# A final norm without GpSimd products: one more residual sum on the tensor engine, and the eight tiles in a new order

## The chip, the core and the metric

The kernel runs on one core of one Trainium2 chip. The metric is the time of one execution on the device in microseconds (us); the figure to be moved is the median of repeated executions.

## What is computed

One layer of a diffusion backbone on 1024 latent tokens of width 1024 (a token mixer, then an expert-choice mixture of 16 experts), and at the end an RMS norm. What matters here is the end: the experts' outputs are summed into the tokens, and each token is normed.

```python
def expert_choice_ffn(h, w_r, w1, w3, w2):
    ...
    gate, idx = lax.top_k(jnp.swapaxes(aff, 1, 2), cap)      # cap = 128 tokens for each expert
    xe = h[bidx, idx]
    hid = jax.nn.silu(jnp.einsum('becd,edf->becf', xe, w1)) * jnp.einsum('becd,edf->becf', xe, w3)
    ye = jnp.einsum('becf,efd->becd', hid, w2) * gate[..., None].astype(h.dtype)
    return jnp.zeros_like(h).at[bidx, idx].add(ye)

def rmsnorm(x, g):
    xf = x.astype(jnp.float32)
    y = xf * lax.rsqrt(jnp.mean(xf * xf, axis=-1, keepdims=True) + EPS)
    return (y * g.astype(jnp.float32)).astype(x.dtype)

x = x + g2x * expert_choice_ffn(hx2, w_router[l], w1[l], w3[l], w2[l])
...
return rmsnorm(x, final_g)
```

## The kernel before

Nearly all of the time goes to the 16 experts, one after the other. Their weights stream in over one DMA queue as pieces of 1 MB (tile `raw`); ScalarE (ACT) rounds each piece to `hi` (line 107), VectorE (DVE) takes the rest as `lo` (line 109), and TensorE (PE) multiplies both with the split activations (`up`, lines 1258 to 1262, and `down`, lines 1301 to 1307). The outputs of experts 0 to 14 are scattered into the token array `x2d` in DRAM by an indirect DMA that adds (line 1317). Each engine works its queue in the order in which the program is written, and waits on semaphores in between.

The last expert is treated otherwise, and its end is what the change touches. While it still runs, the four pieces of `x2d` (two tiles of 128 tokens each) are loaded into `xf` (line 1386). Its output `ye` is split into `yh` (ACT, line 1393) and `yl` (DVE, line 1394). Then each of the eight tiles `t` of 128 tokens by 1024 goes through four steps:

- `spread(t, add)`: PE multiplies a one-hot matrix `ohT` with `yh` and `yl` (lines 1406 and 1407), so that the expert's rows land at their tokens, in two PSUM banks `fp` of 512 columns. With `add`, PE puts the token's own row `xf` in first, through a product with the identity (line 1405), and the sum `x` then stands in PSUM. There are six banks of this kind, so three tiles can be in them at a time.
- `residual(t)`: for tiles without `add`, DVE adds the two banks to `xf` (line 1414, twice 128x512).
- `square(t)`: ACT squares and sums the row (line 1424) and takes the root (line 1429, with line 1428 ahead of it where the row comes in two halves).
- `finish(t)`: DVE takes the reciprocal `r` (line 1441) and writes the output `fo`, which SP's queue stores (line 1449). There are two ways to write it: `scalar_tensor_tensor` computes `x * r * fg` in one instruction (line 1448); or, where `gains(t)` has had GpSimd (POOL) multiply `x` by the gains `fg` (line 1436), DVE only multiplies by `r` with a `tensor_scalar` (line 1446).

Before, tiles 2, 3 and 4 have their sum made on PE, tiles 0, 1, 5, 6 and 7 on DVE, and tiles 1, 5, 6 and 7 have their gains product on GpSimd. Nothing but the order of the calls at the end of the program sets the order of the work.

Of the kernel before, what the change touches and what calls it, by code (L numbers as in the profile page):

```python
# [7 lines left out]
F32 = mybir.dt.float32  # L8
# [4 lines left out]
OP = mybir.AluOpType  # L13
# [3 lines left out]
D = 1024  # L17
# [3 lines left out]
P = 128  # L21
# [24 lines left out]
def hybrid_layer(ctx, tc, x, c, ctxt, c_ctx, w_mod, b_mod, norm1_g, norm2_g, w_in, sgu_g, sgu_w,  # L46
# [3 lines left out]
    V, A, PE, G = nc.vector, nc.scalar, nc.tensor, nc.gpsimd  # L50
# [19 lines left out]
    def bank(shape, name, small=0):  # L70
        return banks[small].tile(shape, F32, name=name, tag="bk")

    def raw(shape, dt, name):
        return rawp.tile(shape, dt, name=name, tag="raw")
# [96 lines left out]
    ident = con.tile([P, P], F32, name="ident")  # L171
# [129 lines left out]
    for k in range(8):  # L301
        hi = p0.tile([P, 2048], F32R, name="mhi", bufs=2)
        lo = p0.tile([P, 2048], F32R, name="mlo", bufs=2)
        for c0, n_ in (((0, 4),) if k < 7 else ((0, 1), (1, 1), (2, 1), (3, 1))):
            sl = slice(c0 * 512, (c0 + n_) * 512)
            A.activation(hi[:, sl], wm0[k][:, sl], AF.Copy)
            V.tensor_sub(lo[:, sl], wm0[k][:, sl], hi[:, sl])
            for w in (hi, lo):
                for n in range(c0, c0 + n_):
                    PE.matmul(pm[n], cs4[:, k, :], w[:, n * 512:(n + 1) * 512],  # L310
                              start=(k == 0 and w is hi), stop=(k == 7 and w is lo))
# [18 lines left out]
    for j in range(16):  # L330
# [8 lines left out]
                           op0=OP.add, op1=OP.mult)  # L339
# [204 lines left out]
    XS = {}  # L544
# [299 lines left out]
    p = bank([P, 4, P], "ws")  # L844
# [304 lines left out]
    for h in range(2):  # L1149
        sl = slice(h * 512, (h + 1) * 512)  # L1150
# [195 lines left out]
    for e in range(NE):  # L1346
# [24 lines left out]
        else:  # L1371
# [5 lines left out]
            fg = mp.tile([P, D], F32, name="fg", tag="xe", bufs=2)  # L1377
# [13 lines left out]
    for n in range(2):  # L1391
        sl = slice(n * 512, (n + 1) * 512)
        A.activation(yh[:, sl], ye[:, sl], AF.Copy)
        V.tensor_sub(yl[:, sl], ye[:, sl], yh[:, sl])
    FP, XS = {}, {}

    def spread(t, add):

        v = xf[t // 4][:, t % 4]
        FP[t] = [bank([P, 512], "fp") for _ in range(2)]  # L1400
        for n in range(2):
            sl = slice(n * 512, (n + 1) * 512)
            p = FP[t][n]
            if add:
                PE.matmul(p, ident, v[:, sl], start=True, stop=False)
            PE.matmul(p, ohT[:, t * P:(t + 1) * P], yh[:, sl], start=not add, stop=False)
            PE.matmul(p, ohT[:, t * P:(t + 1) * P], yl[:, sl], start=False, stop=True)
        if add:
            XS[t] = FP[t]

    def residual(t):
        v = xf[t // 4][:, t % 4]
        for n in range(2):
            V.tensor_add(v[:, n * 512:(n + 1) * 512], v[:, n * 512:(n + 1) * 512], FP[t][n])
        XS[t] = [v]

    fo = {}

    def square(t):
        if t not in fo:  # L1420
            fo[t] = raw([P, 2, D], F32, "fo")
        w = D // len(XS[t])
        for n, v in enumerate(XS[t]):
            A.activation(fo[t][:, 1, n * w:(n + 1) * w], v, AF.Square, accum_out=fs[:, n, t:t + 1])
        m = epst
        if len(XS[t]) > 1:
            m = fs[:, 0, t:t + 1]
            A.activation(m, m, AF.Identity, bias=epst, scale=1.0 / D)
        A.activation(fs[:, 2, t:t + 1], fs[:, len(XS[t]) - 1, t:t + 1], AF.Sqrt, bias=m, scale=1.0 / D)

    GM = set()

    def gains(t):

        fo[t] = raw([P, 2, D], F32, "fo")
        G.tensor_tensor(fo[t][:, 0], XS[t][0], fg, op=OP.mult)
        GM.add(t)

    def finish(t):
        o, r = fo[t][:, 0], fs[:, 2, t:t + 1]  # L1440
        V.reciprocal(r, r)
        w = D // len(XS[t])
        for n, v in enumerate(XS[t]):
            sl = slice(n * w, (n + 1) * w)
            if t in GM:
                V.tensor_scalar(o, o, r, None, op0=OP.mult)
            else:
                V.scalar_tensor_tensor(o[:, sl], v, r, fg[:, sl], op0=OP.mult, op1=OP.mult)
        nc.sync.dma_start(out[t * P:(t + 1) * P], o)

    for t, add in ((0, False), (1, False), (5, False), (2, True), (3, True)):
        spread(t, add)
    residual(0)
    square(0)
    residual(1)
    gains(1)
    square(1)
    finish(0)
    residual(5)
    gains(5)  # L1460
    spread(6, False)
    spread(7, False)
    square(2)
    finish(1)
    square(5)
    finish(2)
    spread(4, True)
    residual(6)
    gains(6)
    square(3)  # L1470
    finish(5)
    finish(3)
    square(6)
    residual(7)
    gains(7)
    finish(6)
    square(4)
    finish(4)
    square(7)
    finish(7)  # L1480


# [29 lines left out]
```

## Time and profile before

| | us |
|---|---|
| median of 3 runs | 1621.77 |
| lowest and highest | 1614.16, 1622.4 |
| the profiled execution | 1619.82 |
| its span | 1617.7 |
| PE busy, share of the span | 1531.9 (95%) |
| DVE busy | 1386.6 (86%) |
| ACT busy | 1089.8 (67%) |
| POOL busy | 144.6 (9%) |

A profile is of one execution. The span runs from its first to its last recorded instruction, and 2.1 us lie around it. Times inside the trace count from the span's start. The busy shares are means over the whole span; the stretch that the change touches is the last 32 us, and there the shares are others. In a timeline a row gives an instruction's start and how long it took, and in square brackets how long its engine had been idle and what ended that. [...]

### The profile page before, as it was taken

How to read it: one execution, taken by the hardware profiler on the slowest of the kernel's cores; microseconds unless marked ns; L12 is line 12 of the kernel's file. 1: busy time of each engine (PE TensorE's matmuls, PEld its weight loads, DVE VectorE, ACT ScalarE, POOL GpSimd, SP SyncE). 2: the span in 40 equal slices, each digit the busy share in tenths (PEclk: the TensorE clock that was granted, in tenths of full speed). 3: DMA queues.
4: the chain of work that ended last, by engine and by line, in shares of the span. 5: the costliest groups of instructions: out<-in, count | busy, mean ns of one | idle time of the engine just before them, and what ended most of it. 6: DMA issues, size and time to landing. Idle time of an engine off the chain costs nothing.

```text
span 1617.7 us, 19119 instructions
## 1 busy us (share of the span) xinstructions
PE 1531.9 (95%) x7288; PEld 1257.4 (78%) x7288; DVE 1386.6 (86%) x1322; ACT 1089.8 (67%) x990; POOL 144.6 (9%) x126
## 2 busy tenths in 40 slices
PE   5899989999769999999999999999999999999996
PEld 2687779888657888888888888888888888887784
DVE  6668788886878898998989889898998989889797
ACT  6577654722347877777777777868777787777873
POOL 2411121000010010010100001010010100001002
PEclk8899999998879999999999999999999999999998
DMA  9110147435659999999999999999999999999855
GB/s 383 35 36 30 66 151 228 171 127 207 233 214 357 381 375 356 396 366 397 381 365 381 372 378 381 380 385 357 387 370 388 387 371 373 370 384 377 325 173 207
DMA packets 85947, 485.30 MB, mean 300 GB/s; under 512 B 11224, under 2 KB 20064, under 8 KB 35680
## 3 DMA queue, kind: packets, MB, share of 16 engines
q1 hardware_dynamic: 80896, 466.72, 74.9%
q0 software_dynamic: 4864, 17.34, 4.3%
q8 instruction: 57, 0.93, 0.2%
q14 instruction: 34, 0.28, 0.0%
q10 hardware_dynamic: 96, 0.03, 0.0%
HBM read 463.61 MB, written 20.45 MB: 299 GB/s over the span
## 4 chain that ended last, share of the span: by engine, by line
PE 67%; DVE 16%; ACT 7%; DMA 7%; issue 3%; POOL 1%; SPq 0%; DVEq 0%; POOLq 0%; ACTq 0%
PE h L1258 12%; PE h L1262 12%; PE h L1260 12%; PE ye L1304 7%; PE ye L1301 7%; PE ye L1307 7%; DMA raw<-in_w_dram 3%; DVE lo L109 3%; ACT hi L107 2%; PE hp L1285 2%; DVE ring L404 1%; DMA ring<-in_w_mod_dram 1%; DVE sg L1279 1%; PE pw L925 1%; PE pw L927 1%
## 5 line engine op out<-in xcount | busy, mean ns | idle before, releaser
L109 DVE TENSOR_TENSOR lo<-raw,hi 128x2048 fp32r<-128x2048 f32 x383 | 871.0, 2292 | 116.3 <-ACT hi L107 112.1
L107 ACT ACTIVATE hi<-raw 128x2048 fp32r<-128x2048 f32 x384 | 737.3, 1922 | 215.5 <-PE h L1262 150.9
L1258 PE MATMUL h<-hi,xth 128*128 128x512 f32 x1024 | 292.6, 400 | 3.6 <-ACT sg L1269 1.2
L1260 PE MATMUL h<-lo,xth 128*128 128x512 f32 x1024 | 279.9, 390 | 1.9 <-DVE lo L109 1.9
L1262 PE MATMUL h<-hi,xtl 128*128 128x512 f32 x1024 | 279.7, 390 | 0.0
L1258 PEld LDWEIGHTS h<-hi,xth 128*128 128x128 f32 x1024 | 187.8, 188 | 50.6 <-DVE sg L1279 12.6
L1260 PEld LDWEIGHTS h<-lo,xth 128*128 128x128 f32 x1024 | 192.4, 188 | 42.6 <-DVE lo L109 2.8
L1262 PEld LDWEIGHTS h<-hi,xtl 128*128 128x128 f32 x1024 | 192.4, 188 | 40.6
L1301 PE MATMUL ye<-hi,hth 128*128 128x512 f32 x512 | 158.0, 390 | 0.0
L1304 PE MATMUL ye<-lo,hth 128*128 128x512 f32 x512 | 157.8, 389 | 0.0
L1307 PE MATMUL ye<-hi,htl 128*128 128x512 f32 x512 | 157.6, 389 | 0.0
L1317 POOL DMA_INDIRECT x2d<-ye,ix x15 | 50.6, 3374 | 790.0 <-DVE ye L1314 790.0
L1304 PEld LDWEIGHTS ye<-lo,hth 128*128 128x128 f32 x512 | 96.0, 188 | 20.3 <-DVE lo L109 0.3
L1307 PEld LDWEIGHTS ye<-hi,htl 128*128 128x128 f32 x512 | 96.1, 188 | 20.0
L1301 PEld LDWEIGHTS ye<-hi,hth 128*128 128x128 f32 x512 | 95.8, 188 | 19.6
L1269 ACT ACTIVATE sg<-h 128x512 f32<-128x512 f32 x64 | 69.7, 1109 | 0.1
L1288 ACT ACTIVATE hth<-hp 128x512 fp32r<-128x512 f32 x64 | 35.0, 596 | 42.3 <-PE hp L1285 42.3
L377 PE MATMUL pu<-hxh,wh 128*128 128x512 f32 x128 | 51.0, 399 | 1.0 <-ACT g1row L738 1.0
L1236 POOL DMA_INDIRECT xe<-hx2d,ix x16 | 17.7, 1106 | 382.9 <-DVE gate L1231 367.5
L379 PE MATMUL pu<-hxl,wh 128*128 128x512 f32 x128 | 50.6, 395 | 0.0
L378 PE MATMUL pu<-hxh,wl 128*128 128x512 f32 x128 | 50.6, 395 | 0.0
L404 DVE SCALAR_TENSOR_TENSOR ring<-ring,cs 128x1024 f32<-128x1024 f32 x28 | 42.2, 1506 | 8.0 <-DMA ring<-in_w_mod_dram 7.3
(346 smaller groups left out, 1897.5 us busy)
## 6 DMA issues: line engine op xcount, KB each, us to landing
raw<-in_w_dram SPq DMA_DIRECT2D x383, 1024.0 KB, 7.6
ring<-in_w_mod_dram SPq DMA_DIRECT2D x32, 512.0 KB, 4.9
wmod<-in_w_mod_dram SPq DMA_DIRECT2D x8, 1024.0 KB, 10.6
wraw<-in_w_in_dram SPq DMA_DIRECT2D x6, 1024.0 KB, 11.9
xh<-in_x_dram SPq DMA_DIRECT2D x4, 1024.0 KB, 15.7
wor<-in_w_out_dram SPq DMA_DIRECT2D x4, 1024.0 KB, 8.5
xr<-in_x_dram SPq DMA_DIRECT2D x8, 512.0 KB, 4.1
x2d<-xr SPq DMA_DIRECT2D x8, 512.0 KB, 3.5
```

The lines of the kernel that those rows point to most:

```text
L107: A.activation(hi, s, AF.Copy)
L109: eng.tensor_tensor(lo, s, hi, op=OP.subtract)
L377: PE.matmul(p, w[0][:, k], act[0][:, k], start=(k == 0), stop=False)
L378: PE.matmul(p, w[1][:, k], act[0][:, k], start=False, stop=False)
L404: V.scalar_tensor_tensor(macc, row, cs[:, k, 0:1], macc, op0=OP.mult, op1=OP.add)
L1258: PE.matmul(pt[b], hi[:, k], wh[:, b * 512:(b + 1) * 512], start=(k == 0), stop=False)
L1260: PE.matmul(pt[b], hi[:, k], wl[:, b * 512:(b + 1) * 512], start=False, stop=False)
L1262: PE.matmul(pt[b], lo[:, k], wh[:, b * 512:(b + 1) * 512], start=False, stop=(k == 7))
L1269: A.activation(s.rearrange("t j p -> t p j"), pt[b].rearrange("t (p j) -> t p j", j=4), AF.Silu)
L1301: PE.matmul(pt[n], hi[:, j], wh[:, j2 * 1024 + n * 512:j2 * 1024 + n * 512 + 512], start=st_, stop=False)
L1304: PE.matmul(pt[n], hi[:, j], wl[:, j2 * 1024 + n * 512:j2 * 1024 + n * 512 + 512], start=False, stop=False)
L1307: PE.matmul(pt[n], lo[:, j], wh[:, j2 * 1024 + n * 512:j2 * 1024 + n * 512 + 512], start=False, stop=en)
```

## The change

`gains` and its products on GpSimd are gone, and every tile is finished by `scalar_tensor_tensor`. Tile 6 joins tiles 2, 3 and 4, whose sums are made on PE; tiles 0, 1, 5 and 7 stay with DVE. The identity products of `spread` become a step of their own, `carry(t)`, which can stand ahead of the one-hot products; `carry(2)` stands first of all. The calls stand in a new order.

```diff
-    def spread(t, add):
+    def carry(t):
 
         v = xf[t // 4][:, t % 4]
         FP[t] = [bank([P, 512], "fp") for _ in range(2)]
         for n in range(2):
+            PE.matmul(FP[t][n], ident, v[:, n * 512:(n + 1) * 512], start=True, stop=False)
+
+    def spread(t):
+
+        add = t in FP
+        if not add:
+            FP[t] = [bank([P, 512], "fp") for _ in range(2)]
+        for n in range(2):
             sl = slice(n * 512, (n + 1) * 512)
             p = FP[t][n]
-            if add:
-                PE.matmul(p, ident, v[:, sl], start=True, stop=False)
             PE.matmul(p, ohT[:, t * P:(t + 1) * P], yh[:, sl], start=not add, stop=False)
             PE.matmul(p, ohT[:, t * P:(t + 1) * P], yl[:, sl], start=False, stop=True)
         if add:
...
     def square(t):
-        if t not in fo:
-            fo[t] = raw([P, 2, D], F32, "fo")
+        fo[t] = raw([P, 2, D], F32, "fo")
...
-    GM = set()
-
-    def gains(t):
-
-        fo[t] = raw([P, 2, D], F32, "fo")
-        G.tensor_tensor(fo[t][:, 0], XS[t][0], fg, op=OP.mult)
-        GM.add(t)
-
...
         for n, v in enumerate(XS[t]):
             sl = slice(n * w, (n + 1) * w)
-            if t in GM:
-                V.tensor_scalar(o, o, r, None, op0=OP.mult)
-            else:
-                V.scalar_tensor_tensor(o[:, sl], v, r, fg[:, sl], op0=OP.mult, op1=OP.mult)
+            V.scalar_tensor_tensor(o[:, sl], v, r, fg[:, sl], op0=OP.mult, op1=OP.mult)
         nc.sync.dma_start(out[t * P:(t + 1) * P], o)
 
-    for t, add in ((0, False), (1, False), (5, False), (2, True), (3, True)):
-        spread(t, add)
+    carry(2)
+    for t in (0, 1, 2):
+        spread(t)
     residual(0)
     square(0)
     residual(1)
-    gains(1)
     square(1)
+    spread(5)
+    square(2)
     finish(0)
     residual(5)
-    gains(5)
-    spread(6, False)
-    spread(7, False)
-    square(2)
+    carry(3)
+    spread(3)
     finish(1)
     square(5)
     finish(2)
-    spread(4, True)
-    residual(6)
-    gains(6)
+    carry(4)
+    spread(4)
     square(3)
     finish(5)
+    carry(6)
+    spread(6)
+    square(4)
     finish(3)
+    spread(7)
     square(6)
+    finish(4)
     residual(7)
-    gains(7)
+    square(7)
     finish(6)
-    square(4)
-    finish(4)
-    square(7)
     finish(7)
```

On PE, where the last expert's products end and the tail begins, there stood before (the numbers tell buffers apart; `xf_12111` holds tiles 2 and 3, and in brackets stands what an instruction waits for):

```order
L1307 MATMUL ye_12120<-hi_12201,htl_12103 128x512
L1406 MATMUL fp_12250<-yh_12244,ohT_11789 128x512 [waits Activation_49]
L1407 MATMUL fp_12250<-yl_12245,ohT_11789 128x512 [waits DVE_49]
L1406 MATMUL fp_12251<-yh_12244,ohT_11789 128x512 [waits Activation_49]
L1407 MATMUL fp_12251<-yl_12245,ohT_11789 128x512 [waits DVE_49]
```

and now:

```order
L1307 MATMUL ye_12120<-hi_12201,htl_12103 128x512
L1402 MATMUL fp_12250<-xf_12111,ident_120 128x512 [waits DMAHW0_49]
L1402 MATMUL fp_12251<-xf_12111,ident_120 128x512
L1412 MATMUL fp_12254<-yh_12244,ohT_11789 128x512 [waits Activation_49]
L1413 MATMUL fp_12254<-yl_12245,ohT_11789 128x512 [waits DVE_49]
L1412 MATMUL fp_12255<-yh_12244,ohT_11789 128x512 [waits Activation_49]
L1413 MATMUL fp_12255<-yl_12245,ohT_11789 128x512 [waits DVE_49]
```

The identity products of tile 2, which wait for a load alone, have moved ahead of the first one-hot products.

On DVE, from the first reciprocal on, there stood before (`xf_12110` is tiles 0 and 1, `xf_12112` tiles 4 and 5, `xf_12113` tiles 6 and 7; `fp` is a PSUM bank):

```order
L1441 RECIPROCAL fs_12114<-fs_12114 128x1 [waits Activation_49]
L1448 SCALAR_TENSOR_TENSOR fo_12286<-xf_12110,fs_12114,fg_11791 128x1024 [waits DVE_49]
L1414 TENSOR_TENSOR xf_12112<-xf_12112,fp_12262 128x512 [waits DMAHW1_49,PE_49]
L1414 TENSOR_TENSOR xf_12112<-xf_12112,fp_12263 128x512 [waits PE_49]
L1441 RECIPROCAL fs_12114<-fs_12114 128x1 [waits Activation_49]
L1446 TENSOR_SCALAR fo_12291<-fo_12291,fs_12114 128x1024 [waits DVE_49,Pool_49]
L1441 RECIPROCAL fs_12114<-fs_12114 128x1 [waits Activation_49]
L1448 SCALAR_TENSOR_TENSOR fo_12314<-fp_12268,fs_12114,fg_11791 128x512 [waits DVE_49]
L1448 SCALAR_TENSOR_TENSOR fo_12314<-fp_12269,fs_12114,fg_11791 128x512
L1414 TENSOR_TENSOR xf_12113<-xf_12113,fp_12302 128x512 [waits DMAHW2_49,PE_49]
```

and now:

```order
L1438 RECIPROCAL fs_12114<-fs_12114 128x1 [waits Activation_49]
L1442 SCALAR_TENSOR_TENSOR fo_12272<-xf_12110,fs_12114,fg_11791 128x1024 [waits DVE_49]
L1420 TENSOR_TENSOR xf_12112<-xf_12112,fp_12280 128x512 [waits DMAHW1_49,PE_49]
L1420 TENSOR_TENSOR xf_12112<-xf_12112,fp_12281 128x512 [waits PE_49]
L1438 RECIPROCAL fs_12114<-fs_12114 128x1 [waits Activation_49]
L1442 SCALAR_TENSOR_TENSOR fo_12277<-xf_12110,fs_12114,fg_11791 128x1024 [waits DVE_49]
L1438 RECIPROCAL fs_12114<-fs_12114 128x1 [waits Activation_49]
L1442 SCALAR_TENSOR_TENSOR fo_12286<-fp_12250,fs_12114,fg_11791 128x512 [waits DVE_49]
L1442 SCALAR_TENSOR_TENSOR fo_12286<-fp_12251,fs_12114,fg_11791 128x512
```

The `tensor_scalar` with its wait for POOL has become a `scalar_tensor_tensor` that waits for DVE's own reciprocal alone, and the residual of tile 6 (the last row of before) is gone from DVE.

On PE, at the end of its queue, there stood before the one-hot products of tile 7's second half and then tile 4:

```order
L1406 MATMUL fp_12309<-yh_12244,ohT_11789 128x512 [waits DVE_49]
L1407 MATMUL fp_12309<-yl_12245,ohT_11789 128x512
L1405 MATMUL fp_12328<-xf_12112,ident_120 128x512 [waits DMAHW1_49,DVE_49]
L1406 MATMUL fp_12328<-yh_12244,ohT_11789 128x512
L1407 MATMUL fp_12328<-yl_12245,ohT_11789 128x512
L1405 MATMUL fp_12329<-xf_12112,ident_120 128x512 [waits DVE_49]
```

and now `carry` and `spread` of tile 6 and `spread` of tile 7:

```order
L1402 MATMUL fp_12330<-xf_12113,ident_120 128x512 [waits DMAHW2_49,DVE_49]
L1402 MATMUL fp_12331<-xf_12113,ident_120 128x512 [waits DVE_49]
L1412 MATMUL fp_12330<-yh_12244,ohT_11789 128x512
L1413 MATMUL fp_12330<-yl_12245,ohT_11789 128x512
L1412 MATMUL fp_12331<-yh_12244,ohT_11789 128x512
L1413 MATMUL fp_12331<-yl_12245,ohT_11789 128x512
L1412 MATMUL fp_12347<-yh_12244,ohT_11789 128x512 [waits DVE_49]
L1413 MATMUL fp_12347<-yl_12245,ohT_11789 128x512
```

Tile 6 has identity products now, and tile 7 has moved to the end. The waits for DVE are for a bank to come free: tile 6 gets the banks that `finish(2)` reads, tile 7 those that `finish(3)` reads.

## Rows read from the trace of the kernel before

**Rows 1.** Waits, 1584 to 1620: engine and line, whom for, us in total, times, longest.

```profile
DVE xf L1414 <- PE fp L1407: 0.6, 3, 0.3
```

**Rows 2.** Timeline of DVE, 1584 to 1620: start us, length us, instruction.

```profile
1588.31 0.69 DVE L1414 TENSOR_TENSOR xf<-xf,fp 128x512 f32<-128x512 f32 x1
...
1591.58 0.15 DVE L1441 RECIPROCAL fs<-fs 128x1 f32<-128x1 f32 x1
1591.77 3.49 DVE L1448 SCALAR_TENSOR_TENSOR fo<-xf,fs,fg 128x1024 f32<-128x1024 f32 x1
...
1596.64 2.89 DVE L1446 TENSOR_SCALAR fo<-fo,fs 128x1024 f32<-128x1024 f32 x1
1599.45 0.15 DVE L1441 RECIPROCAL fs<-fs 128x1 f32<-128x1 f32 x1
1599.63 1.41 DVE L1448 SCALAR_TENSOR_TENSOR fo<-fp,fs,fg 128x512 f32<-128x512 f32 x2
1600.96 1.27 DVE L1414 TENSOR_TENSOR xf<-xf,fp 128x512 f32<-128x512 f32 x2
1602.15 0.16 DVE L1441 RECIPROCAL fs<-fs 128x1 f32<-128x1 f32 x1
...
1612.45 0.15 DVE L1441 RECIPROCAL fs<-fs 128x1 f32<-128x1 f32 x1
1612.71 0.75 DVE L1446 TENSOR_SCALAR fo<-fo,fs 128x1024 f32<-128x1024 f32 x1
```

**Rows 3.** Timeline of POOL in the same stretch, the first two products of four.

```profile
1591.81 2.37 POOL L1436 TENSOR_TENSOR fo<-xf,fg 128x1024 f32<-128x1024 f32 x1 [21.15 <-DVE fs L1441]
1596.59 2.39 POOL L1436 TENSOR_TENSOR fo<-xf,fg 128x1024 f32<-128x1024 f32 x1 [2.41 <-DVE fs L1441]
```

**Rows 4.** Whole kernel, groups by form on DVE: busy us, mean ns | idle before.

```profile
L979 DVE SCALAR_TENSOR_TENSOR hx<-tm,ss,SH2row 128x1024 f32<-128x1024 f32 x7 | 8.9, 1271 | 0.1
```

**Rows 5.** Timeline of DVE, 330 to 348: one instruction of L979 and the next.

```profile
331.13 1.28 DVE L979 SCALAR_TENSOR_TENSOR hx<-tm,ss,SH2row 128x1024 f32<-128x1024 f32 x1
332.33 0.69 DVE L802 TENSOR_TENSOR yl<-uT,yh 128x512 fp32r<-128x512 f32 x1
```

**Rows 6.** Timeline of ACT, 1584 to 1620.

```profile
1596.49 1.06 ACT L1424 ACTIVATE fo<-xf 128x1024 f32<-128x1024 f32 x1 [0.32 <-DVE xf L1414]
...
1597.87 0.58 ACT L1424 ACTIVATE fo<-fp 128x512 f32<-128x512 f32 x1
...
1599.33 0.29 ACT L1429 ACTIVATE fs<-fs 128x1 f32<-128x1 f32 x1
```

**Rows 7.** Timeline of PE, 1584 to 1620.

```profile
1585.15 0.61 PE L1307 MATMUL ye<-hi,htl 128*128 128x512 f32 x2
1587.05 0.49 PE L1406 MATMUL fp<-yh,ohT 128*128 128x512 f32 x1 [1.28 <-ACT yh L1393]
...
1592.13 1.02 PE L1405 MATMUL fp<-xf,ident 128*128 128x512 f32 x2
...
1593.45 1.02 PE L1405 MATMUL fp<-xf,ident 128*128 128x512 f32 x2
...
1597.41 0.40 PE L1406 MATMUL fp<-yh,ohT 128*128 128x512 f32 x1
1597.64 0.40 PE L1407 MATMUL fp<-yl,ohT 128*128 128x512 f32 x1
```

**Rows 8.** Windows of 1 us: busy us (instructions) of PE, PEld, DVE, ACT, POOL; PEclk; DMA.

```profile
1590.00:1591.00 1.00, 1.00 (x4) 0.81 (x3) 0.71 (x2) 1.00 (x2) 0.00 (x0) 0.50 0.00 0
...
1597.00:1598.00 1.00, 1.00 (x6) 0.82 (x5) 1.00 (x1) 0.97 (x4) 1.00 (x1) 1.00 0.41 168
```

**Rows 9.** The four loads of line 1386: duration ns of the issue, first and last start; issue to landing.

```profile
L1386 SPq DMA_DIRECT2D xf<-x2d x4: 377/420/557, 1575.4 to 1576.9; - x4
...
DMA to landing us min/median/max: 4.9/8.6/12.4
```

**Rows 10.** The stores of line 1449: issue to landing.

```profile
DMA to landing us min/median/max: 2.6/2.6/3.0
```

## The prediction

> **What bounds the kernel now.** Over the whole span TensorE is busy 95% and nothing in the change reaches the experts' loops: the first instruction that differs stands behind the last product of the last expert. So I read only the last 32 us, in this order. First the waits of that stretch [rows 1]: DVE's residual sums wait for PE three times, 0.6 us in all, and no other wait of DVE behind the first residual is listed. DVE is thus the engine that sets the end from 1588.31 on; its last instruction ends at 1612.71 + 0.75 = 1613.46 [rows 2], and 4.24 us later the span of 1617.7 us is over. Then DVE's timeline [rows 2] beside GpSimd's [rows 3], to see what fills these 25.15 us. The reader is to see that the same instruction has two lengths there. The last `tensor_scalar` takes 0.75 us, the one of tile 1 takes 2.89. The finish of tile 0, a `scalar_tensor_tensor` of 128x1024, takes 3.49 us, where seven of the same form elsewhere take 1.27 [rows 4]. Each long one lies over a GpSimd product: tile 0's runs from 1591.77 to 1595.26, the product from 1591.81 to 1594.18; tile 1's from 1596.64 to 1599.53, the product from 1596.59 to 1598.98 [rows 2, 3]. That is no wait for data: tile 0 uses no product, and the product that tile 1 needs was done at 1594.18; the one that runs beside tile 1 is tile 5's. Both end 0.55 to 1.1 us behind the product, so DVE stands still for as long as GpSimd multiplies.
>
> **The change part by part.** What DVE does from its first reciprocal on is counted by the distance from one start to the next, since these instructions overlap a little. A reciprocal takes 1599.63 - 1599.45 = 0.18; a finish out of PSUM, in two halves, 1600.96 - 1599.63 = 1.33; a residual in two halves 1602.15 - 1600.96 = 1.19 [rows 2]. A whole `scalar_tensor_tensor` from SBUF with no GpSimd beside it is shown elsewhere: 332.33 - 331.13 = 1.20, and 1.28 to its end [rows 5].
>
> *Removed: four products on GpSimd.* Off the path by themselves, since DVE never waits for their data, but each blocks DVE. *Changed: four finishes* (tiles 1, 5, 6, 7) by `scalar_tensor_tensor` in place of `tensor_scalar`. *Removed from DVE: the residual of tile 6.* After the first reciprocal DVE has, for all eight tiles: 8 x 0.18 = 1.44, four finishes out of PSUM 4 x 1.33 = 5.32, four from SBUF 4 x 1.20 = 4.80, and residuals 5 and 7, 2 x 1.19 = 2.38. The sum is 13.94, and 0.08 more to the end of the last. Before, the same stretch took 1613.46 - 1591.58 = 21.88. The difference, 7.9 us, is the main term. Taken apart it is 2.2 for tile 0 (3.41 to 1.20 between starts), 3.2 for tiles 1 and 5, 2.6 for tile 6 with its residual, 0.3 for the gap between reciprocal and finish, less 0.5 for tile 7, whose 0.75 becomes 1.28.
>
> [...]
>
> *Added on PE: one more identity sum, and two steps in another place.* One bank with an identity product takes 1593.45 - 1592.13 = 1.32 us at the full clock, and a one-hot product 1597.64 - 1597.41 = 0.23 [rows 7], so an identity product costs 1.32 - 0.46 = 0.86. Now there are 8 x 0.86 + 32 x 0.23 = 14.2 us of PE work, against 6 x 0.86 + 7.36 = 12.5 before. `carry(2)`, 1.7 us, waits only for the second of four loads, issued at 1575.4 to 1576.9 and landing after 8.6 us in the median, so by about 1585 [rows 9], and fits where PE stood idle: the last expert product has been issued at 1585.15 + 2 x 0.23 = 1585.6, and the first one-hot product came at 1587.05 behind an idle time of 1.28 [rows 7]. It may push that product by 0.3 us, but the one behind it waits for `yl` anyway, so I cost it at nothing. PE then runs from 1585.6 through about 1600, nearly without a gap. Its cover is DVE, which is busy until 1605. If the cover were gone, the whole extra sum (1.7 us) would be paid.
>
> *The clock.* [...] With `carry(2)` in the gap I expect it to stay up. Then the residuals of tiles 0 and 1 are not paced by PE, and the first reciprocal comes up to 0.4 us earlier; with the clock as before, at 1591.58 as now. I take 0.2.
>
> *ACT.* A square of a row in SBUF takes 1597.87 - 1596.49 = 1.38, of one in PSUM 1599.62 - 1597.87 = 1.75 [rows 6]: 4 x 1.38 + 4 x 1.75 = 12.5 us, from about 1589.7 to 1602.2. DVE needs the roots between 1591.2 and 1604, in the same order, so ACT hides; its slack is 0.5 to 1.3 us at each tile, and it is what comes late next.
>
> *Stores.* SP's queue has the same eight stores in the same order as DVE's finishes, at least 1.4 us apart. Before, the last two were 1 us apart and landings took 2.6 to 3.0 us [rows 10]. I take 0.1 of gain; bounds 0 and 0.4.
>
> The sum is 7.9 + 0.2 + 0.1 = 8.2 us, with the bounds 7.9 and 8.7. DVE's last instruction should end at about 1605.4, the span at 1609.5.
>
> **The rivals.**
>
> *The clock falls for a part of the tail.* PE's 14.2 us grow by up to as much again. Behind PE's last product still come half a residual (0.6), a square with its root (1.5), a reciprocal and a finish (1.5): 3.6 us. PE sets the end once it is done later than 1605.4 - 3.6 = 1601.8, some 2 us later than the full clock gives. [...] For it: the clock did fall within the tail before [rows 8]. Against it: the fall stood behind an idle PE (1.28 us [rows 7]), and the new queue has no such gap until its end.
>
> *Slower: PE becomes the bound altogether.* With the low clock from 1585.6 to the end PE needs 28.4 us, to 1614.0, and DVE ends at 1617.6, 4.2 us later than now. It would take the place of the GpSimd stall as soon as less than a third of PE's work is at the full clock. Against it speaks that the clock was at 1.00 up to the last expert product and that PE now goes on.
>
> *A long finish has another cause.* If the 3.49 us were due to something else, such as ACT's square or the stores beside it, four finishes from SBUF would cost 4 x 2.2 = 8.8 us more than counted, less the 2.2 that tile 0 has now; the gain would be eaten: 0 to 2 us. Against it: the last finish, with ACT idle and a store under way, took 0.75.
>
> *Hand-overs.* The banks of tiles 6 and 7 come free by finishes 2 and 3 on DVE, PE fills them, and DVE and ACT wait for PE. By the sums above tile 7's residual is wanted at 1601 and PE has it at about 1600.3; ACT's slack is 0.5 at the least. If each of two or three hand-overs misses by up to 1 us, 1 to 3 us of the gain are lost: 5 to 7 faster.
>
> **How the numbers follow.** The profiled execution took 1619.82; 8.2 off gives 1611.6. The median of the runs shown is 1.95 above it, which would give 1613.6, and the runs spread by 8 us. I predict the middle, 1612.6, which is 0.57% below the median. A measurement of this kernel can tell about 0.5% (8.1 us) from no change, so the forecast stands at that edge. Chances: the forecast 0.62, of which 0.46 shows as faster by over 0.5% and 0.16 within it; the clock falling in part 0.20 (0.03 and 0.17); hand-overs 0.11 (0.03 and 0.08); another cause of the long finish 0.04 (within, or 0.01 slower); PE as the bound 0.03 (0.02 slower by over 0.5% in an unlucky run, 0.01 within). That is 0.52 faster, 0.45 the same, 0.03 slower. The range goes from the lowest run less the upper bound, 1614.16 - 8.7 = 1605.5, rounded to 1606, to the median less the 3 us of a clock that falls for half of the work, 1618.8, rounded to 1619.
>
> **What would show each step.** No `tensor_scalar` and no GpSimd product behind 1586; the four finishes from SBUF at 1.27 to 1.3 us each; DVE without a gap over 0.5 us from its second reciprocal to its end; from first to last reciprocal and the last finish about 14 us; PEclk at 1.00 from 1585 to 1600 and `carry(2)` ended by 1587.5; 4.1 to 4.2 us between DVE's end and the span's. The prediction is wrong if finishes from SBUF stay above 2 us with GpSimd idle, if PEclk shows 0.50 while PE's queue is full, or if DVE waits for PE or ACT by more than 1 us in all.

## The result

The changed kernel takes 1612.14 us in the median of 20 runs (1607.48 to 1619.37), the kernel before 1621.59 in the median of 20 (1614.16 to 1626.15). The ratio of the means is 0.9947, with a 95% interval of 0.9935 to 0.9959: 8.6 us faster, and between 6.6 and 10.5 (the medians lie 9.45 apart). The forecast was 1612.6.

In the trace of after the span is 1610.4 us, of an execution of 1612.23. The timeline of DVE, from its first instruction on the last expert's output (start, length, instruction):

```profile
1586.35 1.41 DVE L1314 SCALAR_TENSOR_TENSOR ye<-ye,gate,g2row 128x512 f32<-128x512 f32 x2 [3.69 <-PE ye L1307]
...
1589.08 2.54 DVE L1420 TENSOR_TENSOR xf<-xf,fp 128x512 f32<-128x512 f32 x4
1591.97 0.16 DVE L1438 RECIPROCAL fs<-fs 128x1 f32<-128x1 f32 x1 [0.35 <-ACT fs L1434]
1592.17 1.29 DVE L1442 SCALAR_TENSOR_TENSOR fo<-xf,fs,fg 128x1024 f32<-128x1024 f32 x1
1593.37 1.28 DVE L1420 TENSOR_TENSOR xf<-xf,fp 128x512 f32<-128x512 f32 x2
...
1603.28 1.41 DVE L1442 SCALAR_TENSOR_TENSOR fo<-fp,fs,fg 128x512 f32<-128x512 f32 x2
1604.72 0.16 DVE L1438 RECIPROCAL fs<-fs 128x1 f32<-128x1 f32 x1
1604.92 1.28 DVE L1442 SCALAR_TENSOR_TENSOR fo<-xf,fs,fg 128x1024 f32<-128x1024 f32 x1
```

The finish of tile 0, which took 3.49 us [rows 2], takes 1.29, and no other finish from SBUF is longer. From the first reciprocal to the end of the last finish it is 1606.20 - 1591.97 = 14.23 us, where it was 21.88.

I call the stretch from the start of line 1314 to the end of the span the tail. Before, line 1314 started at 1585.58 in that trace, so the tail was 32.12 us; now it is 1610.4 - 1586.35 = 24.05. What lies ahead of the tail differs by some us from one execution to the next for the same program (two traces of the changed kernel, this one and e11, have spans of 1610.4 and 1612.4 us and tails of 24.05 and 24.03), so a tail of one trace says more here than a single time.

PE and the clock, in the timeline of PE and one window of 1 us (columns as in rows 8; PEclk is the clock granted to TensorE, as a share of its full speed):

```profile
1586.37 1.88 PE L1402 MATMUL fp<-xf,ident 128*128 128x512 f32 x4
1587.82 0.67 PE L1412 MATMUL fp<-yh,ohT 128*128 128x512 f32 x1
```
```profile
1590.00:1591.00 1.00, 1.00 (x6) 0.83 (x5) 1.00 (x3) 0.54 (x1) 0.00 (x0) 1.00 0.00 0
```

`carry(2)` fills the gap, and the first one-hot product starts 1.47 us after line 1314, just as before (1587.05 - 1585.58). The clock that stood at 0.50 in the like window [rows 8] is at 1.00, here and in every other window until PE is done. Of the waits between 1576 and the end, two of DVE lie in the tail (columns as in rows 1): the one for the last expert, and 0.3 us for the first root.

```profile
DVE ye L1314 <- PE ye L1307: 3.7, 1, 3.7
...
DVE fs L1438 <- ACT fs L1434: 0.3, 1, 0.3
```

### The profile page after: what moved, and what is told of

The parts are those of the page before. It is cut to its first block, busy times and chain, and to the rows that moved or that the text cites. A ratio compares the mean times of both kernels' runs of the same rounds, so it can differ in the third digit from the quotient of the medians.

```text
span 1610.4 us, 19114 instructions
## 1 busy us (share of the span) xinstructions
PE 1531.9 (95%) x7292; PEld 1260.0 (78%) x7292; DVE 1378.6 (86%) x1321; ACT 1090.1 (68%) x993; POOL 135.2 (8%) x122
## 4 chain that ended last, share of the span: by engine, by line
PE 65%; DVE 17%; ACT 8%; DMA 6%; issue 3%; POOL 0%; SPq 0%; DVEq 0%; POOLq 0%; ACTq 0%
PE h L1260 11%; PE h L1262 11%; PE h L1258 11%; PE ye L1304 7%; PE ye L1301 7%; PE ye L1307 7%; DMA raw<-in_w_dram 4%; DVE lo L109 3%; ACT hi L107 3%; PE hp L1285 2%; DVE ring L404 2%; DVE sg L1279 1%; DMA ring<-in_w_mod_dram 1%; DMA ctx_sb<-in_ctx_dram 1%; PE xp L1246 1%
```

## The experiments

### The products alone, or the order alone

The first kernel (e1) is the one before without its GpSimd products:

```diff
...
-            if t in GM:
-                V.tensor_scalar(o, o, r, None, op0=OP.mult)
-            else:
-                V.scalar_tensor_tensor(o[:, sl], v, r, fg[:, sl], op0=OP.mult, op1=OP.mult)
+            V.scalar_tensor_tensor(o[:, sl], v, r, fg[:, sl], op0=OP.mult, op1=OP.mult)
...
-    gains(1)
...
-    gains(5)
...
-    gains(6)
...
-    gains(7)
```

> The kernel before with the GpSimd products alone taken out: all eight finishes by scalar_tensor_tensor, order and identity sums as before. The tail is counted from DVE's first instruction on the last expert's output (line 1314) to the end of the span: 32.1 us before, 24.1 with the whole change. Theory (DVE stands still while GpSimd multiplies, and that is nearly all of the gain): the finishes from SBUF take 1.3 us and the tail is 25.0 to 26.5 us, 5.6 to 7 shorter than before. Rival 1 (the new order and the identity products in the gap bring the gain): the tail stays at 30 to 32. Rival 2 (the long finish of 3.5 us has another cause than GpSimd): the finishes from SBUF stay above 2 us and the tail at 32 or more.

Measured: 0.9969 of before (0.9951 to 0.9988); the tail is 26.43 us, 5.69 shorter than before. Its DVE timeline:

```profile
1595.80 1.28 DVE L1437 SCALAR_TENSOR_TENSOR fo<-xf,fs,fg 128x1024 f32<-128x1024 f32 x1
...
1600.44 0.17 DVE L1433 RECIPROCAL fs<-fs 128x1 f32<-128x1 f32 x1 [0.77 <-ACT fs L1429]
1600.64 1.41 DVE L1437 SCALAR_TENSOR_TENSOR fo<-fp,fs,fg 128x512 f32<-128x512 f32 x2
1602.31 1.29 DVE L1414 TENSOR_TENSOR xf<-xf,fp 128x512 f32<-128x512 f32 x2 [0.26 <-PE fp L1407]
```

Tile 0's finish takes 1.28 us here with the old order around it. So the products alone made it long, and their removal, with the four finishes that it brings, gives 5.7 of the 8.1 us between these traces (by the ratio 5.0 us, between 2 and 8). In the old order DVE now waits for ACT and PE by about 1 us, 0.77 and 0.26 in these rows. The clock fell in this execution too:

```profile
1594.00:1595.00 1.00, 1.00 (x4) 0.81 (x3) 0.69 (x1) 0.98 (x2) 0.00 (x0) 0.50 0.00 0
```

The second kernel (e2) is the changed one with the products of tiles 1, 5 and 7 put back:

```diff
...
     residual(1)
+    gains(1)
...
     residual(5)
+    gains(5)
...
     residual(7)
+    gains(7)
```

> The changed kernel (new order, identity products ahead, tile 6 summed on PE) with the GpSimd products for tiles 1, 5 and 7 put back, which DVE then finishes by tensor_scalar. Theory (blocking): DVE instructions that lie over a product take as long as the product and 0.5 to 1 us more, and the tail is 28 to 30 us, about halfway or more back to the 32.1 of before. Rival 1 (the order brings the gain): 24 to 25 us, as with the whole change.

Measured: 0.9964 (0.9944 to 0.9984); the tail is 26.87 us, 2.82 longer than with the whole change, which is less than expected. POOL's and DVE's timelines:

```profile
1589.04 2.36 POOL L1442 TENSOR_TENSOR fo<-xf,fg 128x1024 f32<-128x1024 f32 x1 [20.34 <-DVE xf L1420]
1593.82 2.38 POOL L1442 TENSOR_TENSOR fo<-xf,fg 128x1024 f32<-128x1024 f32 x1 [2.41 <-DVE fs L1447]
1603.55 2.35 POOL L1442 TENSOR_TENSOR fo<-xf,fg 128x1024 f32<-128x1024 f32 x1 [7.35 <-DVE fs L1447]
```
```profile
1589.45 3.04 DVE L1454 SCALAR_TENSOR_TENSOR fo<-xf,fs,fg 128x1024 f32<-128x1024 f32 x1
...
1593.87 2.89 DVE L1452 TENSOR_SCALAR fo<-fo,fs 128x1024 f32<-128x1024 f32 x1
...
1598.44 0.75 DVE L1452 TENSOR_SCALAR fo<-fo,fs 128x1024 f32<-128x1024 f32 x1
...
1603.53 1.41 DVE L1454 SCALAR_TENSOR_TENSOR fo<-fp,fs,fg 128x512 f32<-128x512 f32 x2
...
1605.94 0.76 DVE L1452 TENSOR_SCALAR fo<-fo,fs 128x1024 f32<-128x1024 f32 x1 [0.81 <-POOL fo L1442]
```

The first two products cost 3.04 - 1.29 = 1.75 and, against a finish of 1.28, 1.6 us. The third started at 1603.55, over the finish of tile 6, which reads PSUM, and that one kept its 1.41 us. What the third product costs is a plain wait for its data, 0.81 us. Against these costs the `tensor_scalar` of tiles 5 and 7, with no product beside it, takes 0.75 where the finish of the changed kernel takes 1.28, and the span ends 3.80 us behind DVE in place of 4.20. So a product does not block all of DVE. The order does help, but with the products in it a third of the whole gain is lost again.

### What of DVE is blocked, and by what

In the next five kernels GpSimd works beside the changed kernel's tail, on results that nobody reads; the rest is as in the changed kernel. Each was run once, so what is compared is the tail of its trace. First (e5) four products, one behind each residual on DVE:

```diff
+    junk = mp.tile([P, D], F32, name="junk", tag="xtl")
+
+    def beside(v):
+        G.tensor_tensor(junk, v, fg, op=OP.mult)
...
     residual(0)
+    beside(XS[0][0])
...
     residual(1)
+    beside(XS[1][0])
...
     residual(5)
+    beside(XS[5][0])
...
     residual(7)
+    beside(XS[7][0])
```

> The changed kernel with four GpSimd products of 128x1024 added (one behind each of the residuals of tiles 0, 1, 5 and 7), whose results nobody reads and on which no instruction waits. Theory (GpSimd's two-input product itself holds DVE up): DVE instructions with two SBUF inputs that lie over a product get 1 to 2.4 us longer, and the tail grows from 24.1 by 5 to 9 us. Rival (DVE was waiting for the products' data, or long for another reason): no DVE instruction changes its length and the tail stays within 0.5 us of 24.1.

Measured: a tail of 25.93 us, 1.9 more, and not 5 to 9. The four finishes from SBUF do get longer, but by 0.4 to 0.75 us and not by 2.2. Together that is 2.3 us; 0.4 of it comes back behind DVE's end, where the span ends 3.8 us later in place of 4.2. POOL and DVE:

```profile
1592.20 9.04 POOL L1439 TENSOR_TENSOR junk<-xf,fg 128x1024 f32<-128x1024 f32 x3 [19.15 <-DVE xf L1420]
1606.67 2.35 POOL L1439 TENSOR_TENSOR junk<-xf,fg 128x1024 f32<-128x1024 f32 x1 [5.44 <-issue]
```
```profile
1593.80 1.88 DVE L1447 SCALAR_TENSOR_TENSOR fo<-xf,fs,fg 128x1024 f32<-128x1024 f32 x1
1595.61 1.27 DVE L1420 TENSOR_TENSOR xf<-xf,fp 128x512 f32<-128x512 f32 x2
...
1596.99 2.02 DVE L1447 SCALAR_TENSOR_TENSOR fo<-xf,fs,fg 128x1024 f32<-128x1024 f32 x1
...
1600.63 1.68 DVE L1447 SCALAR_TENSOR_TENSOR fo<-xf,fs,fg 128x1024 f32<-128x1024 f32 x1
...
1608.28 1.83 DVE L1447 SCALAR_TENSOR_TENSOR fo<-xf,fs,fg 128x1024 f32<-128x1024 f32 x1
```

The numbers fit one rule to 0.02 us: a finish from SBUF that meets a product ends 1.09 us behind that product's end. The last product ends at 1606.67 + 2.35 = 1609.02; the last finish at 1608.28 + 1.83 = 1610.11. The first product takes 2.40 by its own record and ends at 1594.60; the first finish at 1595.68, 1.08 later. In the other traces with products it is 1.08 to 1.09 as well, wherever more than 0.2 us of the product was left, and 0.55 for the `tensor_scalar` of before and of e2. And it works both ways: three products back to back take 9.04 us in place of 7.1 (2.40, 3.26 and 3.23), since the later two wait for the finish that was let in ahead of them. The two exclude each other and take turns. The residual beside them, with one input in PSUM, keeps 1.27. So what a product costs is the rest of it that a finish meets. Before, product and finish started within 0.05 us of each other, as [rows 2, 3] show for two tiles, because each product was released by the residual behind which DVE went on to the next finish; hence the full 2.2 us. ([rows 3] name the reciprocal that lies between the two; the first product of e2, whose row names the residual, starts ahead of the reciprocal.)

With products of half the width (e6), edited so:

```diff
-        G.tensor_tensor(junk, v, fg, op=OP.mult)
+        G.tensor_tensor(junk[:, :512], v[:, :512], fg[:, :512], op=OP.mult)
```

> As with the four unread products, but each of 128x512. Theory: a product takes about 1.2 us in place of 2.4 and the tail grows by half as much as with the full ones, 2.5 to 4.5 us over 24.1. Rival (a fixed price for each GpSimd instruction, such as a hand-over): the growth is the same as with the full ones.

Measured: a tail of 24.40 us, 0.35 more, far from the 2.5 to 4.5 of the theory. DVE's part from the first reciprocal to its end grew from 14.23 to 14.96, against 16.51 with the full ones, which is a third of that growth and not half. So it is no fixed price for an instruction; and two of the four half products, the first and the last, end before a finish comes by. POOL, and the two finishes that are longer (the others take 1.28):

```profile
1589.37 2.67 POOL L1439 TENSOR_TENSOR junk<-xf,fg 128x512 f32<-128x512 f32 x2 [18.52 <-DVE xf L1420]
1593.85 1.29 POOL L1439 TENSOR_TENSOR junk<-xf,fg 128x512 f32<-128x512 f32 x1 [1.81 <-DVE xf L1420]
1602.89 1.28 POOL L1439 TENSOR_TENSOR junk<-xf,fg 128x512 f32<-128x512 f32 x1 [7.75 <-issue]
```
```profile
1591.62 1.50 DVE L1447 SCALAR_TENSOR_TENSOR fo<-xf,fs,fg 128x1024 f32<-128x1024 f32 x1
...
1594.42 1.80 DVE L1447 SCALAR_TENSOR_TENSOR fo<-xf,fs,fg 128x1024 f32<-128x1024 f32 x1
```

The next (e7) has one input on GpSimd:

```diff
-        G.tensor_tensor(junk, v, fg, op=OP.mult)
+        G.tensor_scalar(junk, v, 2.0, None, op0=OP.mult)
```

> As with the four unread products, but GpSimd does a tensor_scalar of 128x1024: one tensor in, one out. Theory a (any GpSimd work on SBUF holds DVE up): DVE instructions beside it lengthen by as much as it takes. Theory b (only GpSimd's second input collides with DVE's): DVE's lengths stay at 1.3 and 0.75 us and the tail within 0.5 us of 24.1.

Measured: a tail of 23.92 us, and no finish is longer, though all four from SBUF lie over the GpSimd work:

```profile
1586.66 8.50 POOL L1439 TENSOR_SCALAR junk<-xf 128x1024 f32<-128x1024 f32 x3 [19.11 <-DVE xf L1420]
1599.45 2.77 POOL L1439 TENSOR_SCALAR junk<-xf 128x1024 f32<-128x1024 f32 x1 [4.30 <-issue]
```
```profile
1588.31 1.28 DVE L1447 SCALAR_TENSOR_TENSOR fo<-xf,fs,fg 128x1024 f32<-128x1024 f32 x1
...
1590.89 1.28 DVE L1447 SCALAR_TENSOR_TENSOR fo<-xf,fs,fg 128x1024 f32<-128x1024 f32 x1
...
1593.80 1.28 DVE L1447 SCALAR_TENSOR_TENSOR fo<-xf,fs,fg 128x1024 f32<-128x1024 f32 x1
...
1601.05 1.28 DVE L1447 SCALAR_TENSOR_TENSOR fo<-xf,fs,fg 128x1024 f32<-128x1024 f32 x1
```

It came out as theory b has it: this GpSimd work with one input leaves DVE alone. The edit changes GpSimd's instruction together with the number of its inputs. Last, trains of six products from tile 0's residual on; in the first (e8, whose edit is shown) all but one multiply `fg` by itself, in the second (e9) all read tile 0 and `fg`.

```diff
     residual(0)
+    beside(XS[0][0])
+    beside(fg)
+    beside(fg)
+    beside(fg)
+    beside(fg)
+    beside(fg)
```

> The changed kernel with six unread products of 128x1024 back to back on GpSimd from the end of tile 0's residual on, 14 us in all, so that every kind of DVE instruction of the tail meets one. Theory (what is shared is the path of a second SBUF input): the finishes from SBUF (two SBUF tensors) stand still until the train or a product is over, while residuals and finishes with one input in PSUM keep 0.69 and 0.75 us for a half. Rival (GpSimd holds up all of DVE): the PSUM forms and the reciprocals stand still too. The tail grows by 5 to 14 us with either, by 0 if there is no blocking.

> The train of six unread products once more, each now of two different tensors (2.35 us alone). Theory (a product and a DVE instruction with two SBUF inputs exclude each other, and take turns): a finish from SBUF that starts inside a product ends 1.09 us behind that product's end, the next product begins its work only then (its record gets up to 1.1 us longer), finishes from PSUM keep 1.41 and residuals 1.27, and the tail grows by the sum of the rests of products that the four finishes meet: between 0.5 and 4 us. Rival (GpSimd keeps the path for a whole train): the first finish from SBUF stands for 10 us or more.

Measured: tails of 24.58 and 26.33 us. The first train missed its 5 to 14 us, like e5: only two of its four finishes met a product for long, and took 1.88 and 1.53. The second of these met a product of `fg` by itself, so a product that reads one tensor twice holds a finish as well; it ended at 1591.26, the finish 1.09 us later:

```profile
1588.51 12.44 POOL L1439 TENSOR_TENSOR junk<-fg 128x1024 f32<-128x1024 f32 x5
```
```profile
1590.82 1.53 DVE L1447 SCALAR_TENSOR_TENSOR fo<-xf,fs,fg 128x1024 f32<-128x1024 f32 x1
```

The second train grew the tail by 2.3, inside the range written down after e5. The groups of its line 1447, with the lengths in ns as min/median/max:

```profile
L1447 DVE SCALAR_TENSOR_TENSOR fo<-fp,fs,fg x8: 741/748/755, 1593.8 to 1602.0; 128x512 f32<-128x512 f32 x8
L1447 DVE SCALAR_TENSOR_TENSOR fo<-xf,fs,fg x4: 1678/1947/2223, 1588.5 to 1603.0; 128x1024 f32<-128x1024 f32 x4
```

All eight halves out of PSUM keep 0.75 us inside a train; all four from SBUF are 0.4 to 0.95 longer. Even a full train doesn't shut DVE out. The finishes that were held read two SBUF tensors (1.28 to 2.22 us here); the `tensor_scalar` of before, which reads one, was blocked as well (0.75 to 2.89), and by what no run here shows. That GpSimd's side counts too, e7 shows: its `tensor_scalar`, with one input, held no finish (all four took 1.28), while e8's products, which read one tensor twice, did (1.53). Whether the second input or the kind of instruction decides there is open.

### carry(2) and the clock

The changed kernel with `carry(2)` in another place, profiled in two executions (e3 and e10), and the changed kernel itself in one more (e11):

```diff
-    carry(2)
-    for t in (0, 1, 2):
-        spread(t)
+    spread(0)
+    spread(1)
+    carry(2)
+    spread(2)
```

> The changed kernel with carry(2) directly ahead of spread(2) and no longer first. Theory (it fills PE's gap and keeps the clock up): PE is idle for 1.2 to 1.3 us behind the last expert product, the granted clock falls to 0.50 for some us from about 1588 on, the first reciprocal comes 0.2 to 0.4 us later, counted from line 1314, and the tail is 1 to 2.4 us longer than 24.1. Rival (the clock does not depend on that gap): PEclk stays at 1.00 and the tail is at most 0.9 us longer, the PE work that no longer lies in the gap. Rival (PE has slack enough): within 0.3.

> A second look at the kernel with carry(2) behind spread(1). If an idle PE of 1.28 us behind the last expert product brings the clock down by itself, PEclk falls to 0.50 within 3 us of line 1314; in the first look it stayed at 1.00. Theory now (whether it falls depends on where the gap lies by chance): either outcome; with a fall the tail is 0.8 to 1.6 us longer than the 24.8 of the first look, and the first reciprocal 0.2 to 0.4 us later than 5.62 from line 1314.

> A second look at the changed kernel itself. Theory (with carry(2) in the gap the clock has no reason to fall): PEclk 1.00 until PE is done, tail 24.0 to 24.2 us, first reciprocal 5.6 us after line 1314. Rival (its clock was luck): PEclk falls to 0.50 for some us and the tail is 0.6 us longer or more.

Measured: e3, at 0.9967 of before (0.9949 to 0.9985), has a tail of 24.78 us, 0.73 more, with PE idle for 1.28 us as before, and the clock at 1.00 until PE is done: the first rival. In e10, the same kernel, the tail is 26.26 us, and the first reciprocal comes 5.99 us after line 1314 (1592.53 - 1586.54) and not 5.62. A window of 1 us of e3, and one of e10:

```profile
1589.00:1590.00 1.00, 1.00 (x5) 0.47 (x3) 1.00 (x3) 0.87 (x1) 0.00 (x0) 1.00 0.00 0
```
```profile
1590.00:1591.00 1.00, 1.00 (x4) 0.81 (x3) 0.69 (x1) 0.06 (x1) 0.00 (x0) 0.50 0.00 0
```

So behind the gap the clock falls in some executions and not in others; in four traces with the gap (before, e1, e3, e10) it fell in three. A fall costs 26.26 - 24.78 = 1.48 us here. The second trace of the changed kernel, e11, has a tail of 24.03 us, 0.02 from the first, with PEclk at 1.00; in all nine traces with `carry(2)` first (after, e2, e4 to e9, e11) it was at 1.00 in every window of the 15 us behind the start of line 1314. That `carry(2)` is what keeps it up rests on these counts. The length of an idle stretch alone does not decide: in the trace of before the clock fell a second time behind an idle PE of 1.94 us (0.50 from 1602 to 1605), and in e2, with PE idle for 1.6 us from 1596.05, it stayed at 1.00. The window of that fall, and two of e2, in that idle and behind it:

```profile
1603.00:1604.00 1.00, 1.00 (x3) 0.61 (x2) 1.00 (x1) 0.71 (x3) 1.00 (x1) 0.50 0.18 70
```
```profile
1596.63:1597.63 1.00, 0.00 (x0) 0.00 (x0) 0.96 (x4) 1.00 (x4) 0.00 (x0) 1.00 0.00 0
...
1598.63:1599.63 1.00, 1.00 (x4) 0.52 (x3) 0.96 (x3) 0.00 (x0) 0.00 (x0) 1.00 0.76 311
```

In e10 PE worked on at 0.50 and the clock was at 1.00 again from 1593; in the trace of after it fell to 0.50 by 1607, when PE had been done since 1601.3.

### Tile 6 back on DVE

The changed kernel with the residual of tile 6 on DVE again (e4):

```diff
-    carry(6)
     spread(6)
...
     spread(7)
+    residual(6)
     square(6)
```

> The changed kernel with the residual of tile 6 back on DVE: two more 128x512 sums there (1.19 us), a finish from SBUF in place of one from PSUM (0.13 less), and four identity instructions fewer on PE. Theory (DVE is the bound): the tail is 1.0 to 1.3 us longer than 24.1. Rival (PE, with its 14 us of work, has become the bound): the tail is the same or up to 1.7 us shorter.

Measured: 0.9958 (0.9939 to 0.9977), which does not stand apart from the changed kernel's ratio; the tail is 25.17 us, 1.12 more. That is the theory's 1.0 to 1.3: DVE is the bound, and the identity sum on PE is hidden.

## Why the prediction was right

**Main term.** 7.9 us was worked out from the first reciprocal to DVE's end, 21.88 to 13.94 and 0.08. It is 21.88 - 14.23 = 7.65. The missing 0.2 lies at the last tile, where the reciprocal waited for ACT's root (1604.72 - 1603.28 = 1.44 in place of 1.33), and in the reciprocals, 0.19 in the mean in place of 0.18.

**The finish from SBUF** was taken at 1.28 from rows far from the tail [rows 4, 5]; four took 1.29, 1.28, 1.29 and 1.28 (the two not shown above start at 1594.76 and 1597.67).

**Start.** Taken at 0.2 with bounds 0 and 0.4: the first reciprocal came 1591.97 - 1586.35 = 5.62 us after line 1314, where it was 6.00, so 0.38. The clock stayed up, as hoped, and that is what the 0.38 hangs on: e3, with the gap open and the clock up, has 5.62 too, and e10, with the clock down, 5.99. Ahead of the first reciprocal DVE now waits for ACT's root (0.35 us) and no longer for PE.

**Stores.** Taken at 0.1: from DVE's end to the span's end 4.20, where it was 4.24.

**The sum** of these in the tail is 7.65 + 0.38 + 0.04 = 8.07, against 8.2. The ratio gives 8.6; its interval holds 8.07 as well. That the sum comes so near is in part luck, since the start gave 0.2 more than was taken and the main term 0.2 less. And the 0.5 us between the forecast of 1612.6 and the median say little: the forecast was the middle of two values 2 us apart, and the runs spread over 12.

**PE and ACT as cover.** PE's last product starts at 1600.91 and ends at 1601.3, some 0.5 us later than the 1600 of the sum shifted by the 0.77 by which line 1314 comes later; ACT's roots came in time but at the first tile (0.35 us) and the last (0.1).

**The rivals.** A fallen clock in the first part of the tail was seen, but only with the gap open (before, e1, e10); one fall cost 1.5 us, where a fall over half of the work had been put at 8.2 - 3 = 5. No run shows the 3 us of a clock that falls for half of the work, which set the upper end of the range; in e10 it was below 1.00 in the windows from 1589 to 1593, and the tail grew by the 1.5 us. PE as the bound: not seen. Another cause of the long finish: ruled out by e1 and by the unread products of e5. Hand-overs: 0.1 us.

**What was right by luck of the case.** I wrote that DVE stands still for as long as GpSimd multiplies. That is too wide: in these traces only the finish from SBUF (1.28 to 3.49 us) and the `tensor_scalar` (0.75 to 2.89) stood still, and only for the rest of the product that they met. For the four products of before both readings give the same cost, since each began together with such a finish. For e2, e5, e6 and e8 the wide reading put the price too high, from at least 4 in place of 2.8 us (e2) to at least 5 in place of 0.5 (e8).

**The parts of the 8.1 us**, each from its own comparison of two traces: the products 5.7 in the old order, or 2.8 for three of them in the new one; `carry(2)` ahead 0.7, and 1.5 more in an execution where the clock would have fallen; tile 6 on PE 1.1. They are not independent, and what the rest of the order gives by itself was not measured apart.

## What to carry to other kernels

A GpSimd product that nobody waits for stretched a VectorE instruction that reads two SBUF tensors here, at the most by 2.2 us (3.49 in place of 1.28, beside a product of 2.37 that started with it); look for one instruction form with two lengths in the same stretch, and lay GpSimd's timeline beside it. If the product must stay, put it beside VectorE work with an input in PSUM, which kept its 1.41 us in e2 and e9, or give GpSimd an instruction with one input, where the work allows it; e7's cost DVE nothing (four finishes at 1.28). Where PE waits for a value at a change of stage, products that need only what has long been loaded fill the gap; here it was 1.28 us long, and with it filled PEclk was at 1.00 for the 15 us behind the start of line 1314 in nine traces of nine.

## What the runs showed of the hardware

The exclusion works in both directions and by turns: in a train of six products of two tensors (e9), alone 2.35 us each, the longest record is 3.26, and DVE's four finishes from SBUF wait 0.4 to 0.95 us each and no longer.

```profile
L1439 POOL TENSOR_TENSOR junk<-xf,fg x6: 2346/2808/3257, 1586.9 to 1601.8; 128x1024 f32<-128x1024 f32 x6
```

A GpSimd `tensor_scalar` with one input was no faster than a product: 2.77 us for 128x1024 (e7), against 2.35 for the product of two tensors.

The granted clock behind the same idle time of 1.28 us, in the same kernel, fell to 0.50 in one execution (e10) and stayed at 1.00 in another (e3).
